# Corner of the first z pair split later, output slots of two pairs exchanged, one half sum beside its blocks, down sums and residual rows loaded at other steps

## The chip, the core and the metric

The kernel runs on one core of one Trainium2 chip. A core has a matrix engine (TensorE, PE in the profile, with its weight loads as PEld), a vector engine (VectorE, DVE), a scalar engine (ScalarE, ACT), GpSimd (POOL) and SyncE (SP), which work side by side, each with a list of instructions of its own, and wait for each other through semaphores. Here SP does nothing but issue DMA transfers. The metric is the device time of one execution in microseconds. Before the change it is 1954.56 us, the median of three runs (1953.57 to 1956.6).

## The reference

One layer of a bidirectional encoder on 1024 tokens of width 1024, with 16 learned tokens ahead of them, in float32:

```python
h = rmsnorm(h_res, norm1_w)
proj = h @ w_in
(q, k, v, z, b_raw, a_raw, sc_b, sc_c, sc_x, gate_a, gate_b) = split(proj)
o_dn = gated_deltanet_bidir(q, k, v, z, b_raw, a_raw, ...)
y_a = o_dn @ w_branch_dn
y_b = (sc_b * dwconv3(sc_c * sc_x)) @ w_branch_sc
merged = sigmoid(gate_a) * y_a + sigmoid(gate_b) * y_b
h_res = h_res + merged @ w_out
h2 = rmsnorm(h_res, norm2_w)
gu = h2 @ w_gate_up
h_res = h_res + (silu(gu[..., :D_FF]) * gu[..., D_FF:]) @ w_down
out = rmsnorm(h_res, final_norm_w)[:, 16:]
```

The width inside the last block, D_FF, is 2816, which is 22 blocks of 128.

## The kernel before

**Products.** Every float32 operand is split into a high part, rounded to the matrix engine's type by a cast on ScalarE, and a low part, the remainder, by a subtraction on VectorE. A product is then three products: high by high, high by low, low by high. Large products are done by a scheme of seven block products in place of eight (Winograd's form): P1, P2, S2, S1, S3, S4 and TT. Each is 12 matmuls of 128x128 by 128x512 (four k, three terms; line 1576). Within one product the terms that read one of the low parts come last, so that part may come 8 matmuls later than the others: in the first pairs that is the low part of a T tile in S2, S1, S3 and TT of pair 0, and the low part of the sums or of the weights elsewhere.

**The section of the pairs.** After the DeltaNet branch come products of the normed tokens with the columns of z and of the merge gates, two blocks of 128 columns at a time, here called a pair. The first two pairs are columns of z (pairs 0 and 1), and a pair of gate columns follows (2). The order of ScalarE, VectorE and TensorE through pairs 0 to 2 is written out by hand in the string SECTION, step by step; the number behind the underline is the pair. The steps that matter:

- T1h to T4h, T1l to T4l: high (line 1597) and low parts of the token side's combinations, 128x2048 each, loaded through POOL's queue from tx_d. One set serves all pairs.
- b1 to b4: four block sums of a pair's weights, 128x512 each, on VectorE; b1 adds in the place of u1 (the last weight block), so the split of u1 has to come first.
- uh, ul: high (`corner`, line 1634) and low part of u1, read by TT. In pair 0 the tile they go to, w2, lies over memory that the DeltaNet branch's result (vS) took, which is stored to o_d.
- sah, sal: high (line 1642) and low part of the pair's sums for S2 and S4; sbh, sbl: those for S3 and S1, 128x1024 each. In pair 0 the sums for S1 and S3 are split singly: s1h, s1l, s3h, s3l (line 1700), 128x512 each, because there the half sum b1 goes to a tile of its own.
- c1, c2, c3: copies of a finished bank to an output tile (line 1655); a1 to a4: additions of a bank to it (line 1540). S4 adds to the bank that c3 reads.
- h1 to h4: the tanh of the half value (line 1671); s1 to s4 in z pairs: the product that finishes z (line 1674). When both halves of an output tile are finished, it is stored to z_d (line 1677).

An output tile takes a slot of one pool (s4, 128x1024). It is taken at the first step that writes to it, in the order of SECTION, and where the slot's last content is on its way to z_d, the first write waits for that store. The loads of the pairs' weights (raw) and the z_d stores go out on SP in program order.

**The gate and up section.** 22 steps (the loop is at line 2264, j from 0), each of seven products in the order P1, P2, S2, S1, S3, S4, TT, then the activation, stored to act_d. From j = 4 on, each step also takes one block k = j - 4 of w_down, loads it as 128x2048 in two transfers to a single buffer, makes four block sums on VectorE (128x512 each, line 179) and stores them to t_d (`down_sums`, line 2074). From j = 11 on it makes four sums of the activations too (s_d). The instructions here are ordered by a scheduler, which may place those of one step among those of a later or an earlier one, as the buffers allow.

**The down section.** Seven products again, each a loop over 11 blocks k, with four row tiles and 12 matmuls a block (lines 2352 to 2354); operands are loaded on SP (lines 2344 and 2345), cast to a ring of tiles (line 101) and split (line 102). The residual rows, eight tiles of 128x1024 from xn_d, are loaded ahead of its loops (line 2318), four to slots s and four to mA; the first product's end reads the first of them.

Of the kernel before, what the change touches and what calls it, by code (L numbers as in the profile page):

```python
# [48 lines left out]
def encoder_layer(ctx: ExitStack, tc: tile.TileContext, x, meta, norm1_w, w_in, w_ba,  # L49
                  dn_conv_w, A_log, dt_bias, dn_norm_w, sc_conv_w, w_bdn, w_bsc,  # L50
                  w_out, norm2_w, w_gu, w_down, final_w, out):
    nc = tc.nc
# [125 lines left out]
    def sub(out, a, b):  # L178
        nc.vector.tensor_tensor(out=out, in0=a, in1=b, op=ALU.subtract)
# [1431 lines left out]
    def pair_steps(n, j, z=False):  # L1611
# [61 lines left out]
        def finished(k, part, t, y):  # L1673
            nc.vector.scalar_tensor_tensor(out=out_tile(k)[:, part], in0=t, scalar=1.0, in1=y, op0=ALU.add, op1=ALU.mult)
            a[k, "n"] = a.get((k, "n"), 0) + 1
            if a[k, "n"] == 2:
# [16 lines left out]
             "TT": lambda: into("bank", "A22", "T4", True), "h4": last_turn}  # L1693
        if n == 0 and z:
            s1 = first_out[:, right].rearrange("p (k c) -> p k c", c=P)

            def sum_half(x, r):
                sh = first_sums[:, 0, 1, 4 * x:4 * x + 4]
                A_[("S3", "S1")[x]] = sh, first_sums[:, 1, 1, 4 * x:4 * x + 4]
                nc.scalar.copy(sh, r)  # L1700
            half_low = lambda x, r: low_of(first_sums[:, 1, 1, 4 * x:4 * x + 4], r, first_sums[:, 0, 1, 4 * x:4 * x + 4])
            d.update({"b1": lambda: add(s1, u0, u1), "b3": lambda: sub(g0, s1, g0),
                      "s1h": lambda: sum_half(1, s1), "s1l": lambda: half_low(1, s1),
                      "s3h": lambda: sum_half(0, u0), "s3l": lambda: half_low(0, u0),
                      "S4": lambda: into("bank3", "S4", "B22"), "a2": lambda: added("o1", right, "bank3"),
                      "a4": lambda: added("o1", right, "bank2")})
# [11 lines left out]
    def last_pair(n, j):  # L1718
# [29 lines left out]
    SECTION = """  # L1748
        b1_0 b2_0 c1_0 b3_0 b4_0 uh_0 ul_0 sah_0 sal_0 S4_0 T2h a1_0 T2l s1h_0 S2_0 T1h s1l_0 s3h_0 T1l c2_0 S1_0 h_2 T3h l_2 s3l_0 P1_2 T3l c3_0 S3_0
        T4h T4l P2_2 uh_1 c1_1 a3_0 h1_0 ul_1 TT_0 b1_1 b2_1 b3_1 b4_1 sah_1 a2_0 a4_0 sal_1 sbh_1 S2_1 a1_1 h4_0 h2_0 sbl_1 h3_0 c2_1 S1_1 c1_2 s1_0 s2_0 uh_2 c3_1 s3_0 a1_2 ul_2 S3_1 b1_2 b2_2 b3_2 b4_2  # L1750
        h1_1 a3_1 S4_1 sah_2 sal_2 a2_1 sbh_2 sbl_2 TT_1 s4_0 h3_1 h2_1 s1_1 s3_1 h4_1 S2_2 s2_1 s4_1 c2_2 S1_2 h1_2 c3_2 h_3 l_3 S3_2 a3_2 S4_2 a2_2 h3_2 h2_2 TT_2 h4_2
    """
# [320 lines left out]

    def down_sums(k, behind):

        r = ap_.tile([P, 2, D], F32, tag="al1", name=uid("sums"))
        if k == 0:
            nc.scalar.copy(r[:, 0, 0:1], behind[:, 0:1])
        b11, b12, b21, b22 = (r[:, i // 2, 512 * (i % 2):512 * (i % 2) + 512] for i in range(4))
        nc.sync.dma_start(r[:, 0], w_down[k * P:k * P + P, :])  # L2080
        nc.sync.dma_start(r[:, 1], w_down[(HK + k) * P:(HK + k + 1) * P, :])
        for o_, a, b in ((b11, b12, b11), (b12, b22, b12), (b22, b22, b11), (b21, b21, b22)):
            sub(o_, a, b)
        nc.sync.dma_start(t_d[k], r)


# [177 lines left out]
    for j in range(2, NF):  # L2264
# [51 lines left out]
    rows = [s4(D) for _ in range(4)] + [rows2[:, t] for t in range(4)]  # L2316
    for t in range(KT):
        nc.sync.dma_start(rows[t], xn_d[t])
    early = big("mB", [P, 4, D])
# [65 lines left out]
    for n, (a, b, bank) in enumerate((("A11", "B11", bank_x), ("A12", "B21", bank_y), ("S2", "T2", bank_x), ("S1", "T1", bank_y),  # L2385
                                      ("S3", "T3", bank_x), ("S4", "B22", bank_y), ("A22", "T4", bank_x))):
        kept = []
        for k in range(HK):
            hl = operands(a, b, k)
            if n == 6 and k >= HK - NR:  # L2390
                kept.append((k, hl))
                continue
            for t in range(4):
                tile_step(bank, hl, t, k == 0, k == HK - 1)
# [50 lines left out]
```

## Time and profile before

| | us |
|---|---|
| median of three runs | 1954.56 |
| the profiled execution | 1958.33 |
| its span on the core | 1956.6 |
| TensorE busy | 1936.0 (99%) |
| weight loads busy | 1699.5 (87%) |
| VectorE busy | 1483.7 (76%) |
| ScalarE busy | 880.4 (45%) |
| GpSimd busy | 119.3 (6%) |
| mean granted clock of TensorE | 0.996 |

In timeline rows the first number is the start from the beginning of the span, the second the duration, both in microseconds; then engine, line, operation, output and inputs, shape and count. In brackets stands how long the engine had been idle and who released it. Matmuls overlap, so a row of 12 lasts longer than the distance to the next row. A row of the list of waits gives the total, the count and the longest. In a row of windows the stretch is followed by its length, the busy time of each engine, and at the end the granted clock of TensorE, the DMA engines' busy share and GB/s.

### The profile page before, as it was taken

The numbers are of one execution on the slowest core, as the hardware profiler recorded it, in microseconds if no ns is written. First come the engines' busy times: TensorE is split into PE (matmuls) and PEld (weight loads), VectorE is DVE, ScalarE is ACT, GpSimd is POOL, SyncE is SP. The second block draws the span as 40 slices with busy tenths as digits, with TensorE's granted clock in tenths as the row PEclk, the third lists the DMA queues.
The fourth block names the chain that finished last, engine by engine and source line by source line (L and its number), as shares of the span: only waits on it lengthen the run. The fifth ranks groups of instructions, "written<-read, shape, count | busy, mean of one in ns | idle before, by whom it ended". The sixth has DMA issues, their size and how long they took to land.

```text
span 1956.6 us, 32262 instructions
## 1 busy us (share of the span) xinstructions
PE 1936.0 (99%) x11872; PEld 1699.5 (87%) x11872; DVE 1483.7 (76%) x3162; ACT 880.4 (45%) x2029; POOL 119.3 (6%) x424
## 2 busy tenths in 40 slices
PE   9999999999999999999899999999999999999998
PEld 8998999999999999888788888888888788878887
DVE  7888688888998888877765698668667675646575
ACT  6462354636363646444444545235333233324344
POOL 2013101020101010200000000000000000000000
PEclk9999999999999999999899999999999999999999
DMA  4266322323232223368357955232366754577654
GB/s 146 68 173 154 94 87 82 98 82 98 82 98 71 77 60 98 125 209 295 132 208 269 366 190 204 93 123 91 114 237 231 263 174 153 187 272 240 195 177 162
DMA packets 154084, 307.13 MB, mean 157 GB/s; under 512 B 47741, under 2 KB 57398, under 8 KB 150470
## 3 DMA queue, kind: packets, MB, share of 16 engines
q1 hardware_dynamic: 150805, 294.58, 44.7%
q0 software_dynamic: 2528, 9.44, 2.2%
q8 instruction: 93, 1.52, 0.3%
q10 hardware_dynamic: 592, 1.05, 0.1%
q14 instruction: 66, 0.53, 0.1%
HBM read 211.60 MB, written 93.41 MB: 156 GB/s over the span
## 4 chain that ended last, share of the span: by engine, by line
PE 90%; DVE 4%; DMA 3%; ACT 1%; issue 1%; SPq 0%; POOL 0%; DVEq 0%; ACTq 0%; POOLq 0%
PE pm L345 31%; PE pd L1576 13%; PE pe L1576 7%; PE pm L1576 4%; PE pd L931 1%; PE pd L910 1%; PE pd L892 1%; PE pd L895 1%; PE pe L2353 1%; PE pe L2354 1%; PE pe L2352 1%; PE pe L629 1%; PE pd L927 1%; PE pd L2353 1%; PE pd L2354 1%; PE pd L2352 1%
## 5 line engine op out<-in xcount | busy, mean ns | idle before, releaser
L345 PE MATMUL pm<-al,wh 128*128 128x320 f32 (+4 forms) x1248 | 426.4, 347 | 0.0
L345 PE MATMUL pm<-hTh,wh 128*128 128x320 f32 (+4 forms) x1248 | 425.4, 346 | 0.4 <-ACT hTh L1209 0.2
L345 PE MATMUL pm<-hTh,wl 128*128 128x320 f32 (+4 forms) x1248 | 424.5, 345 | 0.0
L345 PEld LDWEIGHTS pm<-hTh,wh 128*128 128x128 f32 x1248 | 233.7, 188 | 10.9 <-ACT hTh L1209 0.9
L345 PEld LDWEIGHTS pm<-hTh,wl 128*128 128x128 f32 x1248 | 233.8, 188 | 10.4 <-POOL wl L1224 0.3
L345 PEld LDWEIGHTS pm<-al,wh 128*128 128x128 f32 x1248 | 233.9, 188 | 9.9
L102 DVE TENSOR_TENSOR al<-raw,ring_h 128x1024 fp32r<-128x1024 f32 x73 | 88.6, 1222 | 65.1 <-ACT ring_h L101 64.2
L101 ACT CAST ring_h<-raw 128x1024 fp32r<-128x1024 f32 x73 | 76.6, 1053 | 108.9 <-PE pe L2354 33.2
L367 DVE SCALAR_TENSOR_TENSOR kq<-ra,wc,kq 128x520 f32<-128x520 f32 x128 | 96.6, 755 | 3.6 <-ACT kq L397 2.0
L917 ACT ACTIVATE w<-pd,small 128x128 f32<-128x128 f32 x128 | 39.9, 363 | 126.8 <-PE pd L910 126.6
L1028 DVE TENSOR_TENSOR wl<-raw,wh 128x512 fp32r<-128x512 f32 x116 | 78.5, 688 | 20.9 <-ACT wh L1031 20.5
L522 DVE TENSOR_TENSOR tm<-fP,fN 128x135 f32<-128x135 f32 (+23 forms) x248 | 72.6, 293 | 7.5 <-DMA fN<-nd 2.0
L526 DVE TENSOR_TENSOR fP<-fP,tm 128x135 f32<-128x135 f32 (+23 forms) x248 | 71.9, 290 | 5.2
L1031 ACT CAST wh<-raw 128x512 fp32r<-128x512 f32 x116 | 68.7, 626 | 3.7 <-issue 3.6
L882 ACT ACTIVATE jk<-NP 128x128 f32<-128x128 f32 x64 | 19.9, 311 | 90.1 <-DVE NP L878 89.1
L2292 ACT ACTIVATE b<-b 128x512 f32<-128x512 f32 x20 | 12.6, 632 | 106.0 <-DVE b L1540 106.0
L1540 DVE TENSOR_TENSOR b<-pd,b 128x512 f32<-128x512 f32 x21 | 14.5, 690 | 52.6 <-PE pd L1576 47.5
L1576 PE MATMUL pd<-b_hl,wh 128*128 128x512 f32 x168 | 51.9, 390 | 0.0
L367 DVE SCALAR_TENSOR_TENSOR vT<-ra,wc,vT 128x520 f32<-128x520 f32 x64 | 48.4, 756 | 3.4 <-ACT vT L397 2.3
L572 ACT ACTIVATE PQ<-PQ,negG 128x128 f32<-128x128 f32 x128 | 43.4, 395 | 16.9 <-DVE PQ L567 16.7
L718 POOL TENSOR_TENSOR tm<-mP,mN 1x15 f32<-1x15 f32 (+7 forms) x120 | 35.4, 295 | 205.9 <-DMA mN<-ndm 197.5
L902 DVE SCALAR_TENSOR_TENSOR r<-pd,negEG,vS 128x128 f32<-128x128 f32 x120 | 36.7, 344 | 13.5 <-PE pd L892 13.0
(705 smaller groups left out, 4842.7 us busy)
## 6 DMA issues: line engine op xcount, KB each, us to landing
raw<-in_w_in_dram SPq DMA_DIRECT2D x70, 512.0 KB
raw<-in_w_gate_up_dram SPq DMA_DIRECT2D x44, 512.0 KB
sums<-in_w_down_dram SPq DMA_DIRECT2D x22, 512.0 KB
t_d<-sums SPq DMA_DIRECT2D x11, 1024.0 KB
raw<-s_d SPq DMA_DIRECT2D x44, 256.0 KB
raw<-t_d SPq DMA_DIRECT2D x44, 256.0 KB
act_d<-b SPq DMA_DIRECT2D x43, 256.0 KB
raw<-act_d SPq DMA_DIRECT2D x33, 256.0 KB
```

The lines of the kernel that those rows point to most:

```text
L101: nc.scalar.copy(hi, src)
L102: nc.vector.tensor_tensor(out=lo, in0=src, in1=hi.bitcast(F32), op=ALU.subtract)
L345: mm(po[:, :n], ww[:, k], f(k)[:, t0:t0 + n], start=i == 0, stop=i == 3 * KT - 1)
L367: nc.vector.scalar_tensor_tensor(out=acc, in0=raw[:, h0 + t:h0 + t + hn], scalar=wc[:, t, col:col + 1], in1=acc, op0=ALU.mult, op1=ALU.add)
L522: nc.vector.tensor_tensor(out=tv, in0=fP[:, 0:r, j:j + 1].broadcast_to([P, r, n]), in1=fN[:, j:j + 1, j + 1:32].broadcast_to([P, r, n]), o ...
L526: nc.vector.tensor_tensor(out=fP[:, 0:r, j + 1:32], in0=fP[:, 0:r, j + 1:32], in1=tv, op=ALU.subtract)
L572: nc.scalar.activation(PQ[:, c, d], PQ[:, c, d], AF.Exp, bias=negG2[:, c, hd:hd + 1])
L917: nc.scalar.activation(w[d], b2[:, 2 + d], AF.Copy, scale=ce[:, c, d:d + 1])
L1028: nc.vector.tensor_tensor(out=u[1][1][:, k], in0=u[2][:, k], in1=u[1][0][:, k].bitcast(F32), op=ALU.subtract)
L1031: nc.scalar.copy(u[1][0][:, k], u[2][:, k])
L1576: mm(po, x[:, k], at(y, k), start=i == 0 and not add_to, stop=i == 11, skip_group_check=add_to)
L2352: mm(bank[t], h_[:, c], h_[:, hi], start=first, stop=False)
```

## The change

Four things change, all of them in order and place. (1) In SECTION uh_0 and ul_0 move from ahead of sah_0 to the steps around T4h; pair 0's ul_0 goes with it. (2) In pair 1 the half sum b1 goes to the output tile o1 as in pair 0, so its S1 and S3 sums are split singly, and uh_1 and ul_1 move behind the block sums. (3) In pairs 1 and 2, c3_1 now stands ahead of c1_2, so they take each other's slots; a1_2 and h1_1 stand later, h3_0 after uh_1. (4) `down_sums` is cut in two: the load of block k is issued at step k + 4 as before, its sums and store at step k + 5; and the loads of the residual rows go from ahead of the down section into the first loop, one a block from k = 3 on.

```diff
--- before.py
+++ after.py
@@ -1691,18 +1691,24 @@
              "S4": lambda: into("bank2", "S4", "B22", True), "a2": lambda: added("o1", right, "bank2"),
              "h2": lambda: half_turn(a["o1"][:, right]),
              "TT": lambda: into("bank", "A22", "T4", True), "h4": last_turn}
+        if z:
+            s1 = lambda: out_tile("o1")[:, right].rearrange("p (k c) -> p k c", c=P)
+
+            def sums_tile():
+                if "s" not in a:
+                    a["s"] = big("b1", [P, 2, 2, KT, P]) if n else first_sums
+                return a["s"]
+
+            def sum_half(x, r):
+                sh, sl = (sums_tile()[:, m, 1, 4 * x:4 * x + 4] for m in range(2))
+                A_[("S3", "S1")[x]] = sh, sl
+                nc.scalar.copy(sh, r)
+            half_low = lambda x, r: low_of(a["s"][:, 1, 1, 4 * x:4 * x + 4], r, a["s"][:, 0, 1, 4 * x:4 * x + 4])
+            d.update({"b1": lambda: add(s1(), u0, u1), "b3": lambda: sub(g0, s1(), g0),
+                      "s1h": lambda: sum_half(1, s1()), "s1l": lambda: half_low(1, s1()),
+                      "s3h": lambda: sum_half(0, u0), "s3l": lambda: half_low(0, u0)})
         if n == 0 and z:
-            s1 = first_out[:, right].rearrange("p (k c) -> p k c", c=P)
-
-            def sum_half(x, r):
-                sh = first_sums[:, 0, 1, 4 * x:4 * x + 4]
-                A_[("S3", "S1")[x]] = sh, first_sums[:, 1, 1, 4 * x:4 * x + 4]
-                nc.scalar.copy(sh, r)
-            half_low = lambda x, r: low_of(first_sums[:, 1, 1, 4 * x:4 * x + 4], r, first_sums[:, 0, 1, 4 * x:4 * x + 4])
-            d.update({"b1": lambda: add(s1, u0, u1), "b3": lambda: sub(g0, s1, g0),
-                      "s1h": lambda: sum_half(1, s1), "s1l": lambda: half_low(1, s1),
-                      "s3h": lambda: sum_half(0, u0), "s3l": lambda: half_low(0, u0),
-                      "S4": lambda: into("bank3", "S4", "B22"), "a2": lambda: added("o1", right, "bank3"),
+            d.update({"S4": lambda: into("bank3", "S4", "B22"), "a2": lambda: added("o1", right, "bank3"),
                       "a4": lambda: added("o1", right, "bank2")})
         if z:
             for i, k, part in ((1, "o1", left), (2, "o1", right), (3, "o2", right)):
@@ -1746,9 +1752,9 @@
         return o1
 
     SECTION = """
-        b1_0 b2_0 c1_0 b3_0 b4_0 uh_0 ul_0 sah_0 sal_0 S4_0 T2h a1_0 T2l s1h_0 S2_0 T1h s1l_0 s3h_0 T1l c2_0 S1_0 h_2 T3h l_2 s3l_0 P1_2 T3l c3_0 S3_0
-        T4h T4l P2_2 uh_1 c1_1 a3_0 h1_0 ul_1 TT_0 b1_1 b2_1 b3_1 b4_1 sah_1 a2_0 a4_0 sal_1 sbh_1 S2_1 a1_1 h4_0 h2_0 sbl_1 h3_0 c2_1 S1_1 c1_2 s1_0 s2_0 uh_2 c3_1 s3_0 a1_2 ul_2 S3_1 b1_2 b2_2 b3_2 b4_2
-        h1_1 a3_1 S4_1 sah_2 sal_2 a2_1 sbh_2 sbl_2 TT_1 s4_0 h3_1 h2_1 s1_1 s3_1 h4_1 S2_2 s2_1 s4_1 c2_2 S1_2 h1_2 c3_2 h_3 l_3 S3_2 a3_2 S4_2 a2_2 h3_2 h2_2 TT_2 h4_2
+        b1_0 b2_0 c1_0 b3_0 b4_0 sah_0 sal_0 S4_0 T2h a1_0 T2l s1h_0 S2_0 T1h s1l_0 s3h_0 T1l c2_0 S1_0 h_2 T3h l_2 s3l_0 P1_2 T3l c3_0 S3_0
+        uh_0 T4h ul_0 T4l P2_2 c1_1 a3_0 h1_0 TT_0 b1_1 b2_1 s1h_1 b3_1 b4_1 sah_1 a2_0 a4_0 sal_1 S2_1 s1l_1 uh_1 a1_1 h4_0 h2_0 s3h_1 c2_1 S1_1 s3l_1 s1_0 s2_0 h3_0 uh_2 c3_1 ul_1 s3_0 ul_2 S3_1 b1_2 b2_2 b3_2 b4_2
+        a3_1 c1_2 S4_1 sah_2 sal_2 a1_2 h1_1 a2_1 sbh_2 sbl_2 TT_1 s4_0 h3_1 h2_1 s1_1 s3_1 h4_1 S2_2 s2_1 s4_1 c2_2 S1_2 h1_2 c3_2 h_3 l_3 S3_2 a3_2 S4_2 a2_2 h3_2 h2_2 TT_2 h4_2
     """
     ru0 = s4()
     first_out = s4()
@@ -2071,18 +2077,21 @@
         nc.scalar.activation(sg, sg, AF.Silu)
         return rg, ru, A_, p1, sg, bank
 
-    def down_sums(k, behind):
+    def down_load(k, behind):
 
         r = ap_.tile([P, 2, D], F32, tag="al1", name=uid("sums"))
         if k == 0:
             nc.scalar.copy(r[:, 0, 0:1], behind[:, 0:1])
-        b11, b12, b21, b22 = (r[:, i // 2, 512 * (i % 2):512 * (i % 2) + 512] for i in range(4))
         nc.sync.dma_start(r[:, 0], w_down[k * P:k * P + P, :])
         nc.sync.dma_start(r[:, 1], w_down[(HK + k) * P:(HK + k + 1) * P, :])
+        return r
+
+    def down_sums(k, r):
+
+        b11, b12, b21, b22 = (r[:, i // 2, 512 * (i % 2):512 * (i % 2) + 512] for i in range(4))
         for o_, a, b in ((b11, b12, b11), (b12, b22, b12), (b22, b22, b11), (b21, b21, b22)):
             sub(o_, a, b)
         nc.sync.dma_start(t_d[k], r)
-
 
     def load_pair(j, spread=False):
 
@@ -2295,8 +2304,10 @@
         mul(sg, b1, sg)
         nc.sync.dma_start(act_d[j][:, 0:512], sg)
         nc.sync.dma_start(act_d[j][:, 512:1024], r2)
+        if 5 <= j <= HK + 4:
+            down_sums(j - 5, loaded)
         if 4 <= j <= HK + 3:
-            down_sums(j - 4, sg)
+            loaded = down_load(j - 4, sg)
         if j >= HK:
 
             s1, s4_ = p1, u2
@@ -2314,8 +2325,6 @@
     nc.sync.dma_start(wfr, final_w.unsqueeze(0).broadcast_to([P, D]))
     rows2 = big("mA", [P, 4, D], F32)
     rows = [s4(D) for _ in range(4)] + [rows2[:, t] for t in range(4)]
-    for t in range(KT):
-        nc.sync.dma_start(rows[t], xn_d[t])
     early = big("mB", [P, 4, D])
     hiw, junk = (t.rearrange("p k c -> p (k c)") for t in (big("b1", [P, 4, 512], F32), big("b2", [P, 4, 512], F32)))
     us = big("b3", [P, 4, 512], F32)
@@ -2387,6 +2396,8 @@
         kept = []
         for k in range(HK):
             hl = operands(a, b, k)
+            if n == 0 and k > 2:
+                nc.sync.dma_start(rows[k - 3], xn_d[k - 3])
             if n == 6 and k >= HK - NR:
                 kept.append((k, hl))
                 continue
```

ScalarE at the start of pair 0, before. `L1634 CAST w` is uh_0, `L1642` sah_0, `L1597` T2, T1, T3 and T4 high, `L1700` s1h and s3h, `L1655` c1_0, c2_0 and c3_0, `L1630` h_2:

```order
L1655 COPY s_2078_12371<-pd_12273 128x512
L1634 CAST w_2088_12387<-s_2077_12370 128x512
L1642 CAST b_2083_12381<-raw_11934 128x1024
L1597 CAST b_2081_12375<-mA_12373 128x2048
L1700 CAST b_2083_12381<-s_2078_12371 128x512
L1597 CAST b_2082_12376<-mA_12373 128x2048
L1700 CAST b_2083_12381<-s_2077_12370 128x512
L1655 COPY s_2078_12371<-pd_12273 128x512
L1630 CAST wh_12452<-raw_12388 128x1024
L1597 CAST mB_12386<-b_2080_12374 128x2048
```

The same place in the changed kernel (line numbers from 1700 on are shifted):

```order
L1655 COPY s_2078_12371<-pd_12273 128x512
L1642 CAST b_2083_12381<-raw_11934 128x1024
L1597 CAST b_2081_12375<-mA_12373 128x2048
L1705 CAST b_2083_12381<-s_2078_12371 128x512
L1597 CAST b_2082_12376<-mA_12373 128x2048
L1705 CAST b_2083_12381<-s_2077_12370 128x512
L1655 COPY s_2078_12371<-pd_12273 128x512
L1630 CAST wh_12450<-raw_12388 128x1024
L1597 CAST mB_12386<-b_2080_12374 128x2048
L1655 COPY s_2098_12470<-pe_12437 128x512
L1634 CAST w_2088_12387<-s_2077_12370 128x512
L1597 CAST mA_12485<-b_2080_12374 128x2048
```

uh_0 stood between c1_0 and sah_0; now sah_0 follows c1_0, and uh_0 stands between c3_0 and the cast of T4.

ScalarE between S1_1 and S4_1, before: the copies to `s_2101`, `s_2107` and `s_2108` are c2_1, c1_2 and c3_1, `L1634` is uh_2, `L1671` h1_1 and `L1642` sah_2. `s_2108` is the slot whose last content, pair 0's first output tile, goes to z_d:

```order
L1655 COPY s_2101_12503<-pd_12316 128x512
L1655 COPY s_2107_12564<-pd_12458 128x512
L1634 CAST w_2088_12387<-raw_12389 128x512
L1655 COPY s_2108_12570<-pe_12551 128x512
L1671 ACTIVATE pm_12591<-s_2101_12503 128x512
L1642 CAST b_2110_12606<-raw_12388 128x1024
```

And in the changed kernel, where `L1671` is h3_0:

```order
L1655 COPY s_2101_12502<-pd_12316 128x512
L1671 ACTIVATE pe_12566<-s_2098_12470 128x512
L1634 CAST w_2088_12387<-raw_12389 128x512
L1655 COPY s_2107_12569<-pe_12549 128x512
L1655 COPY s_2108_12591<-pd_12456 128x512
L1642 CAST b_2109_12605<-raw_12388 128x1024
```

c3_1 (the copy from pe) has moved ahead of c1_2 (the copy from pd) and takes slot 2107; c1_2 takes 2108 and stands directly ahead of sah_2. On SP the z_d store of that tile moves ahead of one raw load, which it stood behind.

VectorE in step 11 of the gate and up section, before. `sums` is the tile of block k = 9; the additions of `pd_16525` and `pm_16568` (line 1540) are those of S3 and S4, the line 1541 rows the two multiplications:

```order
L102 TENSOR_TENSOR wl_16792<-raw_16793,wh_16791 128x1024
L179 TENSOR_TENSOR sums_16912<-sums_16912 128x512 x3
L1540 TENSOR_TENSOR b_2330_15113<-pd_16525,b_2330_15113 128x512
L179 TENSOR_TENSOR sums_16912<-sums_16912 128x512
L1540 TENSOR_TENSOR b_2330_15113<-pm_16568,b_2330_15113 128x512
L1541 TENSOR_TENSOR b_2330_15113<-b_2330_15113 128x512
L1540 TENSOR_TENSOR b_2330_15113<-t_2435_16565,b_2330_15113 128x512
L1541 TENSOR_TENSOR b_2330_15113<-pd_16525,b_2330_15113 128x512
```

And in the changed kernel, where `sums_16777` is block 8 and `sums_16914` block 9:

```order
L102 TENSOR_TENSOR wl_16789<-raw_16790,wh_16788 128x1024
L179 TENSOR_TENSOR sums_16777<-sums_16777 128x512
L102 TENSOR_TENSOR mB_15080<-raw_16653,mB_15080 128x1024
L1540 TENSOR_TENSOR b_2330_15115<-pd_16522,b_2330_15115 128x512
L1540 TENSOR_TENSOR b_2330_15115<-pm_16565,b_2330_15115 128x512
L179 TENSOR_TENSOR sums_16914<-sums_16914 128x512
L1541 TENSOR_TENSOR b_2330_15115<-b_2330_15115 128x512
L1540 TENSOR_TENSOR b_2330_15115<-t_2435_16562,b_2330_15115 128x512
L1541 TENSOR_TENSOR b_2330_15115<-pd_16522,b_2330_15115 128x512
```

The first three subtractions of block 9 stood ahead of the addition of S3; now both additions stand ahead of the first of them, and the others come later.

## The prediction

> **What bounds the kernel now.** I read the busy times first, then the list of what TensorE waits for.
>
> ```profile
> PE 1936.0 (99%) x11872; PEld 1699.5 (87%) x11872; DVE 1483.7 (76%) x3162; ACT 880.4 (45%) x2029; POOL 119.3 (6%) x424
> ...
> PE pe L1576 <- ACT b L1642: 3.6, 1, 3.6
> PE pe L1576 <- ACT s L1655: 2.0, 1, 2.0
> ...
> PE pd L1576 <- DVE b L1540: 1.1, 1, 1.1
> ...
> PE pm L2353 <- DVE al L102: 0.7, 1, 0.7
> ```
>
> TensorE (PE) is busy for 1936.0 of 1956.6 us, so no more than 20.6 us of idle time can be had, apart from time in which it runs at a low clock. Four waits in the middle of the program stand in places that the diff touches. The timeline of TensorE through the first two shows what each costs.
>
> ```profile
> 935.92 0.39 PE L506 MATMUL pm<-hTh,wl 128*128 128x512 f32 x1
> 939.95 0.80 PE L1576 MATMUL pe<-hTh,b 128*128 128x512 f32 x1 [3.64 <-ACT b L1642]
> ...
> 945.24 3.26 PE L1576 MATMUL pd<-b,b 128*128 128x512 f32 x12
> 948.34 2.88 PE L1576 MATMUL pe<-b,b 128*128 128x512 f32 x12
> ...
> 964.99 2.88 PE L1576 MATMUL pe<-b,b 128*128 128x512 f32 x12
> 967.71 2.88 PE L1576 MATMUL pd<-mB,b 128*128 128x512 f32 x12
> 972.58 0.50 PE L1576 MATMUL pe<-hTh,b 128*128 128x512 f32 x1 [2.00 <-ACT s L1655]
> ...
> 979.78 2.88 PE L1576 MATMUL pd<-b,b 128*128 128x512 f32 x12
> 982.50 2.88 PE L1576 MATMUL pe<-b,b 128*128 128x512 f32 x12
> ```
>
> A product of 12 matmuls takes 2.72 us when nothing is late (964.99 to 967.71, 979.78 to 982.50), 0.227 us a matmul. The last L506 matmul leaves the engine free at 935.92 + 0.23 = 936.15; S2_2 starts at 979.78. Between lie 12 products: S4_0, S2_0, S1_0, P1_2, S3_0, P2_2, TT_0, S2_1, S1_1, S3_1, S4_1, TT_1. They need 12 x 2.72 = 32.64 us and took 43.63, so **10.99 us are lost here**. By starts: 3.80 ahead of S4_0, 2.57 within it, 0.38 within S2_0, 0.33 in the six products from 948.34 to 964.99 (16.65 for 16.32), 2.15 ahead of S4_1, and 1.76 in S4_1 and TT_1 (7.20 for 5.44). What lies within products is the clock:
>
> ```profile
> 940.00:945.00 5.00, 5.00 (x12) 3.95 (x13) 5.00 (x5) 4.54 (x4) 0.00 (x0) 0.50 0.37 106
> 973.00:977.00 4.00, 4.00 (x12) 3.14 (x11) 1.48 (x2) 2.44 (x4) 0.00 (x0) 0.57 0.21 41
> ```
>
> After each gap TensorE is busy all the time at a granted clock of 0.50 and 0.57, with 12 matmuls where 5 us hold 22. A gap here costs about twice its length.
>
> Why S4_0 waits stands in the rows of ScalarE (ACT), VectorE (DVE) and the chain:
>
> ```profile
> 934.31 0.59 ACT L1655 COPY s<-pd 128x512 f32<-128x512 f32 x1
> 938.33 0.62 ACT L1634 CAST w<-s 128x512 fp32r<-128x512 f32 x1 [3.43 <-DMA o_d<-vS]
> 938.86 1.04 ACT L1642 CAST b<-raw 128x1024 fp32r<-128x1024 f32 x1
> 939.80 1.90 ACT L1597 CAST b<-mA 128x2048 fp32r<-128x2048 f32 x1
> ...
> 934.09 0.69 DVE L179 TENSOR_TENSOR raw<-raw 128x512 f32<-128x512 f32 x1
> ...
> 934.44 3.79 DMA o_d<-vS
> ...
> 966.31 5.54 DMA z_d<-s
> ...
> 971.95 0.58 ACT L1655 COPY s<-pe 128x512 f32<-128x512 f32 x1 [5.17 <-DMA z_d<-s]
> ```
>
> The corner's cast uh_0 (938.33) writes memory that the o_d stores still read; sah_0, which S4_0 needs, only stands behind it. Its own input b4_0 was done at 934.78. S4_1 waits for c3_1 (971.95), which takes the output slot that the z_d store of pair 0 has to leave.
>
> **The change part by part.**
>
> *Corner.* ScalarE is free at 934.31 + 0.59 = 934.9. With uh_0 gone from ahead of it, sah_0 runs 934.9 to 935.95 and S4_0 can start at 936.15, with no gap. The casts behind it follow at their durations: T2 high (1.90) to 937.85, a half sum (0.62), T1 high (1.89) to 940.2. VectorE adds T2 low, 2.29 us, to 940.2. S2_0 is due at 938.87 and reads T2 low in its last four matmuls, from 940.68; T1 low ends near 943.0, wanted at 943.4. The T2 and T1 tiles must have landed:
>
> ```profile
> 921.45 1.55 POOL L1599 DMA_DIRECT2D mA<-tx_d  x2 [103.25 <-DMA rb<-o_d]
> ...
> mA<-tx_d POOLq DMA_DIRECT2D x2, 1024.0 KB, 6.6
> ```
>
> Issued by 923.0, they land 6.6 us later, before 930, so T2 high is not held. The wait for o_d moves to T3 high, due at about 943, when the stores (end 938.23) are long done. uh_0 now runs near 945.6, ul_0 near 947.5; TT_0 wants them at 952.47. Nothing is late in their place. I take 3.80 + 2.57 + 0.38 = 6.75 us.
>
> *S1 beside its blocks.* In pair 1 one 1024-wide cast and one 1024-wide subtraction become two 512-wide ones each: one row of 0.62 more on ScalarE and one of 0.69 on VectorE, hidden if S2_1 and TT_1 don't wait. By the order of VectorE, b1_1 to b4_1 now come ahead of the corner's low part: b4_1 ends near 953.8, sah_1 (1.05) near 954.9; S2_1 is due at 955.19. The row it lost (0.33 in all) goes. a3_1 ends near 965.7, TT_1 is due at 966.07. With slacks of 0.3 to 0.4 in four places, I charge 0.4 as an estimate; the bounds are 0 and 1.31, both new rows in full on the path.
>
> *Slots.* c3_1 now waits for S1_1 alone (about 961) and S4_1 starts on time at 963.35; the 2.15 + 1.76 = 3.91 us go. c1_2 waits for the z_d store instead, and behind it on ScalarE stand sah_2 and with it S2_2, due at 968.79. s2_0 ends near 960.7 by VectorE's new order; the store of 5.54 us lands at 966.2; c1_2 (0.59) and sah_2 (1.05) end at 967.9: slack 0.9. On SP the store moves ahead of the raw load that uh_3 and pair 3 read; that load, of the same size, goes out at about 961.4 and at the store's 5.54 us lands at 967.0, before uh_3 at 968.8. Next is c3_2, which waits for the store of pair 0's other half: s4_0 near 971.2, plus 5.54 and 0.59, is 977.3, where S4_2 is due at 976.95. I charge 0.4. That term lies between 0 and 3.91, the price of the like wait of S4_1.
>
> *Down sums.*
>
> ```profile
> 1479.44 0.42 SPq L2081 DMA_DIRECT2D sums<-in_w_down_dram  x1
> 1488.13 0.33 SPq L2084 DMA_DIRECT2D t_d<-sums  x1
> 1493.33 0.33 SPq L2080 DMA_DIRECT2D sums<-in_w_down_dram  x1
> ...
> 1484.68 0.69 DVE L179 TENSOR_TENSOR sums<-sums 128x512 f32<-128x512 f32 x1 [4.32 <-DMA sums<-in_w_down_dram]
> ...
> 1543.01 1.42 DVE L179 TENSOR_TENSOR sums<-sums 128x512 f32<-128x512 f32 x2 [0.93 <-DMA sums<-in_w_down_dram]
> 1544.35 0.68 DVE L1540 TENSOR_TENSOR b<-pd,b 128x512 f32<-128x512 f32 x1
> ...
> 1505.32 2.88 PE L1576 MATMUL pd<-b,u_hl 128*128 128x512 f32 x12
> 1541.12 2.88 PE L1576 MATMUL pm<-b,s_hl 128*128 128x512 f32 x12
> 1545.08 3.02 PE L1576 MATMUL pd<-b,u_hl 128*128 128x512 f32 x12 [1.08 <-DVE b L1540]
> ```
>
> TT of step 11 was due at 1541.12 + 2.72 = 1543.84 and started at 1545.08, because the add of S3 (1544.35) stood behind subtractions that waited for their load. In the new order that add and the next stand ahead of the first subtraction of k = 9, so **1.24 us** go. A store takes up to 5.2 us until the next load goes out (1488.13 to 1493.33), a load up to 5.2 (1479.44 to 1484.68), and they share one buffer, so the loads land later in the step than before. The place to watch is k = 6, whose first three subtractions (two need both loads) stand ahead of the add of S3, which must end by 1505.3, when TT is due. The last subtraction of k = 5 ends near 1491.3, behind the two multiplications of its step; 1491.3 + 5.2 + 0.4 + 5.2 = 1502.1 for the landing; two subtractions and the add take 2.0: slack 1.1. What else stands behind them makes operands for the next step.
>
> *Residual rows.*
>
> ```profile
> 1731.42 2.11 SPq L2318 DMA_DIRECT2D s<-xn_d  x4
> ...
> 1743.88 1.35 SPq L2344 DMA_DIRECT2D raw<-act_d  x1
> ...
> 1752.52 0.39 PE L2352 MATMUL pm<-ring_h 128*128 128x512 f32 x1
> 1753.65 0.50 PE L2353 MATMUL pm<-al,ring_h 128*128 128x512 f32 x1 [0.74 <-DVE al L102]
> ...
> 1756.27 0.39 PE L2352 MATMUL pm<-ring_h 128*128 128x512 f32 x1
> ```
>
> One k of the down product takes 2.72 us; this one took 1756.27 - 1752.52 = 3.75. Its operand was issued from 1743.88 on, behind eight row loads and two steps' stores on SP. Now it goes out near 1731, ahead of most rows, so **1.03 us** go. The rows are read at the end of this pass, some 25 us later; the bytes are the same.
>
> *Sum:* 10.99 - 0.4 - 0.4 + 1.24 + 1.03 = 12.5 us. The profiled execution has a span of 1956.6 and took 1958.33, 3.8 above the median of 1954.56; the losses are idle time that doesn't scale, so I take them from the median: **1942.1**.
>
> [...] In front of S4_1 TensorE stood for 2.00 us and the clock fell. [...]
>
> **The rivals.** (a) *A wait takes the place of the one removed:* c1_2 or c3_2 is held 2 us longer than I walked. Against it stands a slack of 0.9; for it, c3_2 has none. Price 3.91, less the 0.4 charged: 1945.6. (b) *The corner gap comes back at S2_0:* the T2 cast waits for older stores, or the casts are late in a row. Then S2_0 stands for 2 us and the slow clock of 2.95 (2.57 + 0.38) remains: 1942.1 + 4.95 = 1947.0. (c) *Down sums and rows give nothing:* 1944.4. (d) *Slower than before:* the late loads of the sums hold the add of S3 in every step in which subtractions stand ahead of it, which the new order has at k = 6, 7, 9 and 10. It decides from a landing 1.1 us later than 1502.1 at k = 6, and 4 us or more for the others. Held by 2.5 us each, with a slow product of 1.76 behind each, that is 4 x 4.26 = 17.0: 1959.1. Against it: loads land within 5.2 us. [...] (e) *The change doesn't do what it says*, sah_0 still waiting for the stores: 1954.6. The waits that it carries in the new order speak against that.
>
> **How the numbers follow.** Forecast 0.62, (a) 0.14, (b) 0.08, (c) 0.08, (d) 0.04, (e) 0.04. The best case keeps all 13.3 us, 1941.3, and the three runs before spread by 1 below their median, so the low end is 1940.3. The high end takes in (a), (b) and (c) and the four slacks lost in full (0.9 more than charged, 1947.9), with the same spread of 1: 1948.9. A difference under 0.2%, 3.9 us, is not to be told from none: below 1950.7 is faster, 0.92, (e) is the same, 0.04, and (d) is slower, 0.04.
>
> **What would show it.** Right: S4_0 starts within 0.3 us of the last L506 matmul; the clock stays at 1.00 from there to S2_2; S2_2 starts some 33 to 34 us after that matmul; c3_1 has no wait for z_d<-s and c1_2 has one; no wait of TensorE for the L1540 add near step 11; the k loop of the down product is even. Wrong: a wait of TensorE above 1 us in the first three pairs or at an add of S3 in the steps k = 6 to 10, above all with a granted clock near 0.5 behind it.

## The result and the profile after

The changed kernel takes **1944.72 us**, the median of six runs (1943.57 to 1945.6); the kernel before, run beside it, takes 1955.07 (1949.92 to 1957.26). The medians differ by 10.35 us; the ratio is 0.9949, with a 95% interval of 0.9936 to 0.9961: 10.0 us less, between 7.6 and 12.5. The forecast was 1942.1, 12.5 us less, with a range of 1940.3 to 1948.9. Two things in these numbers belong together: the profiled execution of the change has a span of 1943.2 us, 13.4 less than the 1956.6 of before, which is more than the medians differ; and the runs of before lie 7 us apart, those of the change 2.

The list of what TensorE waits for, in the changed kernel (total, times, longest):

```profile
PE pd L98 <- POOL ident masks.py:199: 1.5, 1, 1.5
PE pe L629 <- DVE PQ L668: 1.2, 3, 0.5
PE pe L98 <- DVE xr L1195: 1.0, 1, 1.0
PE pd L98 <- DVE ss L162: 0.7, 1, 0.7
PE pd L777 <- issue: 0.3, 1, 0.3
PE pm L345 <- ACT hTh L1209: 0.2, 1, 0.2
```

All four waits that the prediction named are gone, and no new one stands in their place. TensorE's timeline through the pairs:

```profile
936.39 0.40 PE L506 MATMUL pm<-hTh,wl 128*128 128x512 f32 x1
936.62 0.40 PE L1576 MATMUL pe<-hTh,b 128*128 128x512 f32 x1
...
939.35 2.88 PE L1576 MATMUL pd<-b,b 128*128 128x512 f32 x12
...
955.67 2.88 PE L1576 MATMUL pd<-b,b 128*128 128x512 f32 x12
...
966.55 2.88 PE L1576 MATMUL pd<-mA,u_hl 128*128 128x512 f32 x12
969.27 2.88 PE L1576 MATMUL pd<-b,b 128*128 128x512 f32 x12
...
974.71 2.88 PE L1576 MATMUL pd<-mB,b 128*128 128x512 f32 x12
977.46 0.50 PE L1576 MATMUL pe<-hTh,b 128*128 128x512 f32 x1
...
980.31 2.98 PE L1576 MATMUL pd<-mA,w 128*128 128x512 f32 x12
```

S4_0 follows the last L506 matmul at once. From 936.62 to S2_2 at 969.27 it is 32.65 us, the 12 products at full speed; before it was 43.63. From S3_2 (974.71) to TT_2 (980.31) 5.60 us pass for 5.44: the 0.16 is all that S4_2 loses to c3_2. In the stretches behind the old places of the two gaps the windows read a clock of 1.00, with 24 matmuls in 5 us where the first of them held 12 before:

```profile
936.00:941.00 5.00, 5.00 (x24) 4.11 (x23) 4.57 (x4) 5.00 (x5) 0.00 (x0) 1.00 0.96 320
963.00:968.00 5.00, 5.00 (x24) 4.14 (x23) 4.38 (x7) 2.96 (x4) 0.00 (x0) 1.00 0.37 111
```

ScalarE's timeline shows who waits for the stores now. Its rows are sah_0, uh_0, c3_1, c1_2, sah_2 and c3_2; only c1_2 and c3_2 wait for a z_d store, and uh_0 no longer waits for o_d:

```profile
935.35 1.05 ACT L1642 CAST b<-raw 128x1024 fp32r<-128x1024 f32 x1
...
945.98 0.63 ACT L1634 CAST w<-s 128x512 fp32r<-128x512 f32 x1
...
961.30 0.59 ACT L1655 COPY s<-pe 128x512 f32<-128x512 f32 x1 [0.82 <-PE pe L1576]
963.97 0.59 ACT L1655 COPY s<-pd 128x512 f32<-128x512 f32 x1 [2.08 <-DMA z_d<-s]
965.62 1.05 ACT L1642 CAST b<-raw 128x1024 fp32r<-128x1024 f32 x1 [1.07 <-DVE raw L179]
...
976.82 0.59 ACT L1655 COPY s<-pe 128x512 f32<-128x512 f32 x1 [3.52 <-DMA z_d<-s]
```

The wait for the z_d store has gone from c3_1 to c1_2, and costs nothing there: sah_2 behind it waits another 1.07 us for VectorE.

### The profile page after: what moved, and what is told of

The parts are those of the page before. It is cut to its first block, busy times and chain, and to the rows that moved or that the text cites. A ratio compares the mean times of both kernels' runs of the same rounds, so it can differ in the third digit from the quotient of the medians.

```text
span 1943.2 us, 32262 instructions
## 1 busy us (share of the span) xinstructions
PE 1930.3 (99%) x11872; PEld 1696.5 (87%) x11872; DVE 1483.0 (76%) x3163; ACT 881.1 (45%) x2030; POOL 119.6 (6%) x424
## 4 chain that ended last, share of the span: by engine, by line
PE 92%; DVE 3%; DMA 2%; ACT 1%; issue 1%; SPq 0%; POOL 0%; DVEq 0%; POOLq 0%; ACTq 0%
PE pm L345 30%; PE pd L1576 14%; PE pe L1576 7%; PE pm L1576 4%; PE pe L2361 1%; PE pe L2362 1%; PE pe L2363 1%; PE pd L931 1%; PE pd L910 1%; PE pd L892 1%; PE pd L895 1%; PE pd L927 1%; PE pe L629 1%; PE pd L2362 1%; PE pd L2361 1%; PE pd L2363 1%
```

## The experiments

The question is why the medians say some 10 us when the trace shows all 13.4 gone, and what each of the four parts is worth. Ratios are those to the kernel before, run on the same chip, with their 95% intervals; a ratio of 0.0010 is 2.0 us.

**The kernel before again.** No edit.

> The kernel before, unchanged, with a second profile. The forecast of 12.5 us was worked out from one profiled execution of it (span 1956.6); the change's profile is 13.4 us shorter, but the medians of six runs are only 10.3 apart, and the runs of before lie between 1949.9 and 1957.3. Theory A: the gaps of before vary from execution to execution, with the landing of the stores that S4_0 and S4_1 wait for and with the clock behind them. Then this profile has another span, by 1 us or more, and the difference lies in S4_0 to S2_2 (first profile: 43.63 us between the last L506 matmul and S2_2) or in the section of the sums (1.24) and rows (1.03). Theory B: the gaps are the same each time and the difference lies elsewhere, for instance at the start or the end: then the stretch reads 43.6 again, within 0.3.

The median of eleven runs is 1955.18 us, the span of the profile 1954.6. In the 28 runs of before beside it the times go from 1949.7 to 1960.1 us, and the mean granted clock of a run from 0.996 to 0.999. The four runs at 0.996 took 1955.7 to 1960.1 us, the five at 0.999 took 1949.7 to 1956.2 with a median of 1952.6. TensorE's timeline of this profile:

```profile
936.55 0.39 PE L506 MATMUL pm<-hTh,wl 128*128 128x512 f32 x1
940.73 0.80 PE L1576 MATMUL pe<-hTh,b 128*128 128x512 f32 x1 [3.80 <-ACT b L1642]
...
946.02 3.09 PE L1576 MATMUL pd<-b,b 128*128 128x512 f32 x12
948.95 2.88 PE L1576 MATMUL pe<-b,b 128*128 128x512 f32 x12
...
973.07 0.50 PE L1576 MATMUL pe<-hTh,b 128*128 128x512 f32 x1 [1.89 <-ACT s L1655]
...
977.50 2.91 PE L1576 MATMUL pd<-mA,u_hl 128*128 128x512 f32 x12
980.25 2.88 PE L1576 MATMUL pd<-b,b 128*128 128x512 f32 x12
```

The stretch reads 980.25 - 936.78 = 43.47 us, as theory B had it: in this execution the pairs lose as much as in the first. But the wait for the add at step 11 is missing from it, and the one of the down section is 0.3 in place of 0.7. The span is 2.0 us shorter, and what is missing lies at the sums and the rows, as theory A allowed. So this profile alone does not choose for the pairs; the clocks of the runs speak for A, and the next profiles show gaps of other sizes there.

**The corner alone.**

```diff
-        b1_0 b2_0 c1_0 b3_0 b4_0 uh_0 ul_0 sah_0 sal_0 S4_0 ...
+        b1_0 b2_0 c1_0 b3_0 b4_0 sah_0 sal_0 S4_0 ...
-        T4h T4l P2_2 ...
+        uh_0 T4h ul_0 T4l P2_2 ...
```

> The kernel before with the corner's two steps moved in the order string, nothing else. By the sum of the prediction 6.75 us go (3.80 wait, 2.57 and 0.38 slow clock): ratio about 0.9965, and S4_0 starts within 0.3 us of the last L506 matmul. If the gaps of before vary (theory A), the ratio of medians is nearer 0.9975 (5 us). S4_1 still waits about 2 us or more for c3_1, with the slow clock behind it: the store is issued as soon before it as now. Rival: the wait moves to S2_0 or S2_1, and less than 4 us go.

1949.77 us, ratio 0.9971 (0.9959 to 0.9982): 5.7 us, between 3.5 and 8.0. S4_0 no longer waits. S4_1 still does, but look at what follows:

```profile
955.05 3.04 PE L1576 MATMUL pd<-b,b 128*128 128x512 f32 x12 [0.22 <-ACT b L1642]
...
965.27 0.50 PE L1576 MATMUL pe<-hTh,b 128*128 128x512 f32 x1 [1.75 <-ACT s L1655]
...
968.13 2.88 PE L1576 MATMUL pd<-mA,u_hl 128*128 128x512 f32 x12
```

After 1.75 us of waiting S4_1 takes 2.86 us, not 4.46: in this execution the clock did not fall.

**The pair's part alone:** S1 beside its blocks and the exchanged slots, with the corner, the down sums and the rows as before. The first block of the change's diff stands, and of its string:

```diff
-        T4h T4l P2_2 uh_1 c1_1 a3_0 h1_0 ul_1 TT_0 b1_1 b2_1 b3_1 b4_1 sah_1 ... sbh_1 S2_1 ... c1_2 s1_0 s2_0 uh_2 c3_1 ...
+        T4h T4l P2_2 c1_1 a3_0 h1_0 TT_0 b1_1 b2_1 s1h_1 b3_1 b4_1 sah_1 ... S2_1 s1l_1 uh_1 ... s1_0 s2_0 h3_0 uh_2 c3_1 ul_1 ...
-        h1_1 a3_1 S4_1 sah_2 ...
+        a3_1 c1_2 S4_1 sah_2 sal_2 a1_2 h1_1 ...
```

> The kernel before with S1 beside its blocks and the exchanged slots, the corner where it was. By the sum 3.91 us go for S4_1 and up to 0.33 around S2_1: ratio about 0.9979. S4_0 still waits 3.6 us for the cast of the sums. Rival: c1_2 is held by the z_d store so long that S2_2 waits in S4_1's place; then the time is unchanged within 1 us.

1951.52 us, ratio 0.9988 (0.9978 to 0.9997): 2.3 us, between 0.6 and 4.3, where some 4 were expected (ratio 0.9979, just inside the interval). S4_1 and S2_2 have no wait; S4_0's was 5.0 us in its profile, with 1.9 us of slow clock behind.

**The down sums alone.**

```diff
+        if 5 <= j <= HK + 4:
+            down_sums(j - 5, loaded)
         if 4 <= j <= HK + 3:
-            down_sums(j - 4, sg)
+            loaded = down_load(j - 4, sg)
```

> The kernel before with the load and the sums of the down blocks a step apart, nothing else. By the sum 1.24 us go (ratio about 0.9994) and the wait of TensorE for the L1540 add at step 11 is gone. Rival: the subtractions of k = 6 hold the add of S3, with a wait of up to 1 us there, and the ratio is 1.000.

1953.58 us, ratio 0.9993 (0.9984 to 1.0003): by itself this cannot be told from no change. Its profile carries the clearest pair of waits:

```profile
936.66 0.39 PE L506 MATMUL pm<-hTh,wl 128*128 128x512 f32 x1
939.37 0.50 PE L1576 MATMUL pe<-hTh,b 128*128 128x512 f32 x1 [2.32 <-ACT b L1642]
...
942.23 2.88 PE L1576 MATMUL pd<-b,b 128*128 128x512 f32 x12
...
969.11 0.77 PE L1576 MATMUL pe<-hTh,b 128*128 128x512 f32 x1 [1.93 <-ACT s L1655]
...
973.55 2.88 PE L1576 MATMUL pd<-mA,u_hl 128*128 128x512 f32 x12
```

Here the longer wait, ahead of S4_0, is followed by a product of 2.86 us, and the shorter, ahead of S4_1, by one of 4.44. The last section shows from the traces what sets them apart.

**The residual rows alone.**

```diff
-    for t in range(KT):
-        nc.sync.dma_start(rows[t], xn_d[t])
...
+            if n == 0 and k > 2:
+                nc.sync.dma_start(rows[k - 3], xn_d[k - 3])
```

> The kernel before with the residual rows' loads inside the first down loop, nothing else. By the sum 1.03 us go, ratio about 0.9995. But the second profile of before shows only 0.3 us for the wait of TensorE on the split of the down operands, where the first shows 0.7, so the term may be an accident of one execution: then the ratio is 0.9998 or nearer to 1. Rival: the rows now come between operand loads and delay them, with a wait above 0.7 us there.

1954.32 us, ratio 0.9994 (0.9985 to 1.0003): inconclusive by itself too, though the wait in the down section is gone. S4_0 waited longest in this profile, and S4_1's wait of 1.94 us again had no slow clock behind it:

```profile
936.23 0.39 PE L506 MATMUL pm<-hTh,wl 128*128 128x512 f32 x1
942.47 0.79 PE L1576 MATMUL pe<-hTh,b 128*128 128x512 f32 x1 [5.85 <-ACT b L1642]
...
946.66 2.89 PE L1576 MATMUL pd<-b,b 128*128 128x512 f32 x12
...
973.57 0.50 PE L1576 MATMUL pe<-hTh,b 128*128 128x512 f32 x1 [1.94 <-ACT s L1655]
...
976.43 2.88 PE L1576 MATMUL pd<-mA,u_hl 128*128 128x512 f32 x12
```

**The change without its corner.** The changed kernel with uh_0 and ul_0 ahead of sah_0 again.

```diff
-        b1_0 b2_0 c1_0 b3_0 b4_0 sah_0 sal_0 S4_0 ...
+        b1_0 b2_0 c1_0 b3_0 b4_0 uh_0 ul_0 sah_0 sal_0 S4_0 ...
-        uh_0 T4h ul_0 T4l P2_2 c1_1 ...
+        T4h T4l P2_2 c1_1 ...
```

> The changed kernel with the corner's two steps put back where they were. If the parts add up, it is slower than the changed kernel by what the corner alone gained (ratio 0.9971 alone, 5.7 us): ratio to before about 0.9976. If the parts share a gain, it is nearer 0.997.

1949.54 us, ratio 0.9974 (0.9965 to 0.9984). Within the noise the parts add up: the corner is worth 0.9974 - 0.9949 = 0.0025 within the change, 4.9 us, beside 0.0029 alone. This profile shows the tight spot that the prediction named at k = 6, on VectorE and TensorE:

```profile
1500.69 1.42 DVE L179 TENSOR_TENSOR sums<-sums 128x512 f32<-128x512 f32 x2 [1.50 <-DMA sums<-in_w_down_dram]
1502.02 0.68 DVE L1540 TENSOR_TENSOR b<-pd,b 128x512 f32<-128x512 f32 x1
...
1502.76 3.06 PE L1576 MATMUL pd<-b,u_hl 128*128 128x512 f32 x12 [0.29 <-DVE b L1540]
```

The subtractions wait for their load, the add of S3 behind them is late, and TT of that step with it, by 0.29 us.

**Corner and slots, without S1 beside its blocks.**

```diff
-        ... S1_1 c1_2 s1_0 s2_0 uh_2 c3_1 s3_0 a1_2 ul_2 ...
+        ... S1_1 s1_0 s2_0 uh_2 c3_1 s3_0 ul_2 ...
-        h1_1 a3_1 S4_1 sah_2 sal_2 a2_1 ...
+        h1_1 a3_1 c1_2 S4_1 sah_2 sal_2 a1_2 a2_1 ...
```

(on top of the corner's edit.)

> The kernel before with the corner's steps moved and the slots exchanged, but S1 of pair 1 not beside its blocks. The corner alone left waits of 0.22 us at S2_1 and 1.75 us at S4_1. By the prediction's sum the exchange takes the 1.75 and the slow clock where it comes, and the 0.22 plus the slow matmuls behind it (0.3 in all) stay: ratio about 0.9958, and 1950 - 2.5 = 1947.3 us. If S1 beside its blocks is what lets sah_1 come in time for more than that, S2_1 waits 0.6 us or more and TT_1 too.

1947.00 us, ratio 0.9956 (0.9943 to 0.9968), near the 1947.3 expected: 2.8 us below the corner alone, though the two intervals overlap. S4_1 has no wait; S2_1's 0.22 us stays.

**The wait kept, the standing still taken away.** Ahead of S4_0 come 14 matmuls on finished operands, into the bank that S4_0 then starts afresh.

```diff
+            def warmed():
+                a["bank3"] = psz()
+                for i in range(14):
+                    mm(a["bank3"], gh[:, i % 4], mov["B22"][0][:, i % 4], start=True, stop=True)
+                into("bank3", "S4", "B22")
...
-                      "S4": lambda: into("bank3", "S4", "B22"), ...
+                      "S4": warmed, ...
```

> The kernel before with 14 further matmuls on operands that are ready, ahead of S4_0, into the bank that S4_0 then starts afresh; they leave the result unchanged and run inside the wait for the corner. It keeps TensorE from standing still and leaves the wait as it is. Theory A: behind the wait the clock falls in some executions and not in others, and that is the part of the 6.75 us that the corner's removal does not return in the median. Then the granted clock stays at 1.00 behind S4_0, the wait for the cast stays (2.3 to 5.0 us less 3.2 of matmuls), the median falls by 1 to 2.5 us, and the runs spread less than the 8 to 10 us of before. Theory C: the clock's fall is not a matter of the wait but of the products themselves: then S4_0 still takes 4 to 5 us and the time stays.

1953.18 us, ratio 0.9988 (0.9980 to 0.9997): 2.3 us less with 14 matmuls more. The runs go from 1951.4 to 1956.4.

```profile
935.80 3.33 PE L1699 MATMUL pe<-hTh,wh 128*128 128x512 f32 x14
939.84 0.50 PE L1576 MATMUL pe<-hTh,b 128*128 128x512 f32 x1 [0.70 <-ACT b L1642]
...
942.69 2.88 PE L1576 MATMUL pd<-b,b 128*128 128x512 f32 x12
```

S4_0 still starts 939.84 - 935.80 = 4.04 us after it could, and then takes 2.85 us at a granted clock of 1.00. So the slow product is a matter of standing still, not of the product, and theory C falls.

**The changed kernel again, and without one part each.** The next four share their runs of before, but the differences that count are those between them, since their runs spread by 2 to 3 us.

> The changed kernel, unchanged, as the yardstick of the next three: its runs spread by 2 us where those of before spread by 10. Theory A: with no wait of TensorE above 0.5 us in the middle of the program the clock has nothing to fall behind, so all runs read 0.999 and lie within 3 us; median 1944 to 1945.5. If the spread comes from elsewhere, these runs spread as those of before.

1945.14 us, ratio 0.9942 (0.9929 to 0.9955), runs from 1943.4 to 1945.7 and every clock at 0.998 or 0.999.

The changed kernel with `down_sums` whole, as before:

```diff
-        if 5 <= j <= HK + 4:
-            down_sums(j - 5, loaded)
         if 4 <= j <= HK + 3:
-            loaded = down_load(j - 4, sg)
+            down_sums(j - 4, sg)
```

> The changed kernel with the sums of the down blocks as before. The prediction's term is 1.24 us, and the first profile lost 1.68 us there (two steps took 39.76 us instead of 38.08). But five later profiles with the old order took 38.08 to 38.33, so by now I expect 0 to 0.3 us more than the changed kernel. Should the term be real, it is 1.2 us or more.

1945.51 us: 0.4 us more, which is within the noise. In its profile the wait is there again, in step 11:

```profile
1527.55 3.01 PE L1576 MATMUL pd<-b,s_hl 128*128 128x512 f32 x12 [0.63 <-ACT b L2291]
1530.40 2.88 PE L1576 MATMUL pm<-b,s_hl 128*128 128x512 f32 x12
1534.13 3.02 PE L1576 MATMUL pd<-b,u_hl 128*128 128x512 f32 x12 [0.85 <-DVE b L1540]
```

The changed kernel with the rows loaded ahead of the down loops:

```diff
+    for t in range(KT):
+        nc.sync.dma_start(rows[t], xn_d[t])
...
-            if n == 0 and k > 2:
-                nc.sync.dma_start(rows[k - 3], xn_d[k - 3])
```

> The changed kernel with the residual rows loaded ahead of the down loops as before. The prediction's term is 1.03 us; the wait reads 0.2 to 0.8 us in eight profiles, so I expect 0.5 to 1.0 us more than the changed kernel, with the wait on the split of the down operand back. Rival: the loads of the rows cost as much where they are now, and the time is the same.

1945.96 us: 0.8 us more, not clear of the noise either, and the wait is back, 0.33 us in this execution:

```profile
1739.31 0.50 PE L2364 MATMUL pm<-al,ring_h 128*128 128x512 f32 x1 [0.33 <-DVE al L102]
```

The changed kernel with S1 of pair 1 not beside its blocks, the block of `s1` and `sums_tile` for pair 0 alone again and the string of corner and slots:

```diff
-        ... b1_1 b2_1 s1h_1 b3_1 b4_1 sah_1 ... S2_1 s1l_1 uh_1 ... s3h_1 ... s3l_1 ...
+        ... uh_1 c1_1 a3_0 h1_0 ul_1 TT_0 b1_1 b2_1 b3_1 b4_1 sah_1 ... sbh_1 S2_1 ... sbl_1 ...
```

> The changed kernel without S1 of pair 1 beside its blocks. Corner and slots alone left 0.22 us of wait and some 0.4 us in all around S2_1, so 0.3 to 0.5 us more than the changed kernel. The prediction's own sum says 0.33 for it. If it is what gives the stretch its slack, a wait above 1 us comes at S2_1 or TT_1.

1944.83 us, 0.3 us less than the changed kernel, which such runs cannot tell from none. The wait at S2_1 is back and costs what it did, yet the median doesn't show it:

```profile
955.85 3.06 PE L1576 MATMUL pd<-b,b 128*128 128x512 f32 x12 [0.22 <-ACT b L1642]
```

## Why the prediction was right, and where its sizes were off

**What bounds the kernel, and where it lost: right.** The four waits sat where the list had them and went as a whole. The walk along ScalarE and VectorE gave the order of events, and the times below but for sah_2 within half a microsecond; the profile of the change starts 0.47 us later (936.39 for 935.92), and counted from there:

| step | forecast | measured |
|---|---|---|
| S4_0 after the last L506 matmul | 0.23 | 0.23 |
| start of uh_0 | 945.6 | 945.98 - 0.47 = 945.5 |
| end of sah_2 | 967.9 | 966.67 - 0.47 = 966.2 |
| S2_2 | 968.79 | 968.80 |
| lost at S4_2 to c3_2 | 0.4 | 0.16 |
| lost in the four tight places | 0.4 | 0.0 |

sah_2 came earlier because the z_d store took 3.0 us from its issue (960.92 on SP) to c1_2, not 5.54; c1_2 therefore never was the risk. What sah_2 waited for last was VectorE's block sum, which the prediction's walk to it left out, and it still ended 2.6 us ahead of S2_2. k = 6 was closer than walked. On VectorE and TensorE of the changed kernel:

```profile
1492.89 1.42 DVE L179 TENSOR_TENSOR sums<-sums 128x512 f32<-128x512 f32 x2 [1.07 <-DMA sums<-in_w_down_dram]
1494.22 0.68 DVE L1540 TENSOR_TENSOR b<-pd,b 128x512 f32<-128x512 f32 x1
...
1495.36 2.88 PE L1576 MATMUL pd<-b,u_hl 128*128 128x512 f32 x12
```

The add of S3 ends at 1494.90 and TT starts on time at 1495.36: a slack of 0.46 us, not 1.1; without the corner TT was 0.29 late. None of it grew to the slower rival. The rivals (a), (b), (d) and (e) did not come; (c) is what partly came. That the measured 1944.72 lies beside the 1944.4 of (c) is chance: by the medians below, more than half of what is missing is in the corner and the slots, which (c) left whole.

**The terms, one by one.** The last column is from medians.

| part | forecast, us | measured, us |
|---|---|---|
| corner | 6.75 | 5.7 alone (3.5 to 8.0), 4.9 within the change |
| slots | 3.91 less 0.4 | 2.8 (with the corner against the corner alone, intervals overlapping); 2.3 (0.6 to 4.3) together with S1, without the corner |
| S1 beside its blocks | 0.33 less 0.4 | not to be told from 0 |
| down sums | 1.24 | 0.4, within the noise |
| residual rows | 1.03 | 0.8, not clear of it either |
| all | 12.5 | 10.0 (7.6 to 12.5) |

The measured parts, with the corner alone, sum to 9.7, which is closer to 10.0 than their noise could promise. The last two rows of parts rest on medians of six runs that spread by 2 to 3 us, and are no better than about 1 us; the slots are no better than about 2.

**The step that was mis-sized** is the one from a single profiled execution to the median: "the losses are idle time that doesn't scale, so I take them from the median". That execution was 3.8 us above the median, as the prediction itself noted, and it held three things at once that no later profile holds together: the slow clock behind S4_1, the wait at step 11 and one of the longer waits in the down section. That these make up all of the 3.8 us isn't shown. Three terms were too large by it:

- *Slots:* the price of 3.91 had 1.76 us of slow clock in it. The six profiles in which S4_1 waits (1.75 to 2.00 us) show a slow S4_1 in three (the first of before, the second, the down sums alone: 4.46, 4.43 and 4.44 us) and one at full speed in the other three (the corner, the rows, the warmed one: 2.86 to 2.89). Half of 1.76 less gives about 3.0, which the measured 2.8 and 2.3 allow.
- *Down sums:* the wait of 1.24 us at step 11 is in the first profile, and in the one without the change's sums, but nowhere above 0.2 us in the six others with the old order.
- *Residual rows:* the wait reads 0.7 us in the first profile and 0.2 to 0.8 in those that came after, so the term was too large by less.

*The corner* was sized nearly right in spite of this: wait and slow clock together read 6.75 and 6.73 in the two profiles of before, 7.1, 7.5 and 7.2 in three others, and 2.6 in the one of the down sums alone (working below). That one profile and the interval of 3.5 to 8.0 around 5.7 are all that can be said of the 1 us that is missing.

**The clock behind a wait.** The prediction took the row of a clock that fell after 2.00 us of waiting for what such a wait brings, in the price of S4_1 and in rival (d). The runs bear it out in half of the cases: of the six waits of 1.75 to 2.00 us at S4_1, three were followed by a slow S4_1 (4.43 to 4.46 us) and three by one at full speed (2.86 to 2.89 us). The last section sets beside each wait where it lay against the times at which the clock changed; these lie multiples of 3.41 us apart in the first profile. Taking the row as certain cost the forecast some 0.9 us at S4_1, half of 1.76.

**What is left open.** Why the wait for the o_d stores lasts 2.5 us in one execution and 6.0 in another wasn't tried. Part of the remaining spread of all kernels is not in these stretches: the wait for the first inputs (`xr`, L1195) reads 0.9 us to 2.5 us in the profiles, the changed kernel's own two among them (1.0 and 2.5; the granted clock of those two executions had a mean of 0.999 and 0.998).

## What to carry to other kernels

When an instruction that waits for a store stands ahead of one whose operands are ready, in the same engine's order, look for a place behind, where the store has long landed: here that, and the exchange of two buffers' slots, took away nearly all that the middle of the program lost (32.65 us from S4_0 to S2_2 for 43.63). Before a gap is priced from one profile, set the profiled execution's time beside the median: where it lies above by 3.8 us, some gaps in it may be missing from most executions, and what varies (here S4_1 at 4.46 us or at 2.86, and the wait of 1.24 us at step 11, at most 0.2 us in six other profiles) should enter with its mean over two or three profiles, not its value in one. Removing the waits also narrowed the runs from some 10 us to 2, so the last small terms are better measured against the changed kernel than against the old one.

## What the runs showed of the hardware

Waits of the same length are followed by a halved clock in one execution and by a full one in the next: three of six at S4_1 (1.75 to 2.00 us). In the first profile of before the granted clock reads 0.50 from 939.18 to 946.01, from 973.31 to 976.73 and, behind the last matmul, from 1952.94 on, and 1.00 between. The first two slow stretches last 6.83 and 3.42 us, 27.30 us lie between them and 976.21 between the second and the third, which is 2, 1, 8 and 286 times 3.41. In the second profile the pace of the matmuls goes from 0.43 back to 0.23 us near 946.4, in S2_0, and to 0.43 again near 973.7, with the third matmul of S4_1: 27.3 us again. In these two profiles the clock thus changed at steps of 3.41 us, and not at a wait's end: at 973.31 S4_1 had already been at work again for 0.73 us. The table lays steps of 3.41 us, counted from the ends of each profile's own slow stretches, over the wait ahead of S4_1, and gives the most time that TensorE stood still within one step. Where the ends are read from the pace of the matmuls, in all but the first profile, these times are good to some 0.05 us:

| profile | wait, us | idle within one step, us | S4_1 took, us |
|---|---|---|---|
| before | 2.00 | 2.00 | 4.46 |
| before again | 1.89 | 1.89 | 4.43 |
| down sums alone | 1.93 | 1.93 | 4.44 |
| rows alone | 1.94 | 1.03 | 2.86 |

The clock fell where the whole wait lay within one step, and stayed in the one where a boundary divided it. The corner alone and the kernel with matmuls in the first wait, where S4_1 took 2.86 and 2.89 us behind 1.75 and 1.91 us of waiting, have no slow stretch in these rows to count from. S4_0 agrees: the clock fell behind steps with 2.87, some 2.65 and some 2.1 us of standing still (before, before again, the pair's part alone), and not behind the 1.40 and 0.92 of the down sums alone. One step with 1.91 us, in the rows alone, kept its clock, beside the 1.89 and 1.93 above that did not. As an estimate from these numbers, a wait of 1.9 us falls whole into one step in (3.41 - 1.9) / 3.41 = 0.44 of the cases. No run shifted a wait against these steps on purpose; this is read from the traces alone.

At S4_0 the slow part grows shorter as the wait grows longer, in the five profiles in which the clock fell. Taking for the wait the start of S4_0 less the time at which the last L506 matmul left the engine free, and for the slow clock what S4_0 and S2_0 take above 2.72 us each:

| profile | wait, us | slow clock, us | both |
|---|---|---|---|
| before | 3.80 | 2.95 | 6.75 |
| before again | 3.95 | 2.78 | 6.73 |
| pair's part alone | 5.18 | 1.94 | 7.12 |
| without the corner | 5.51 | 1.71 | 7.22 |
| rows alone | 6.01 | 1.48 | 7.49 |
| down sums alone | 2.48 | 0.14 | 2.62 |

A wait that is longer by 2.2 us (the rows alone against the first profile) costs 0.7 more in all, since less of the work falls into the slow stretch. In the first profile that stretch began 0.77 us ahead of S4_0, while TensorE still stood, and the full clock came back 6.06 us after the work resumed (939.95 to 946.01); with the rows alone it came back after 2.88 (942.47 to 945.35). And 14 matmuls of no use, laid into the wait, left 0.70 us of standing still ahead of S4_0; the clock read 1.00 from 930 to 950 in that profile, and the kernel became 2.3 us faster.
